# The out-projection of a hybrid decoder layer by seven block products, its weight sums formed beside attention

## The chip, the core and the metric

The kernel runs on one core of one Trainium2 chip. The metric is device time in microseconds (us) of one execution of the whole program. TensorE (PE) multiplies, VectorE (DVE), ScalarE (ACT) and GpSimd (POOL) do the rest of the arithmetic, and SyncE (SP) issues every DMA of this kernel.

## The reference, cut to what matters

One layer on 2048 tokens of width 1024: a norm, one input projection for two groups of heads (latent attention with 8 heads of 64, and a gated linear recurrence of width 512), and then one out-projection of both groups' outputs, the residual and a last norm. All in float32.

```python
h = rms_norm(x, ln_g[l])
proj = h @ w_in[l]
q_lat, kv_lat, k_rope, g_mla, hq, hf, hi, g_hg = jnp.split(proj, split_pts, axis=-1)
y_mla = mla_group(...) * jax.nn.silu(g_mla)                 # (1, 2048, 512)
y_hg = hgrn2_group(...) * jax.nn.silu(g_hg)                 # (1, 2048, 512)
y = jnp.concatenate([y_mla, y_hg], axis=-1) @ w_out[l]      # 2048x1024 by 1024x1024
x = x + y.astype(x.dtype)
return rms_norm(x, final_norm_g)
```

## The kernel before

**Precision.** A float32 product is made of three products of split operands (mm3, lines 67 to 70): each operand is a high part, rounded to the matmul's type, and a low part, the rest. Making the pair takes one cast on ACT and one subtraction on DVE or POOL.

**Stages.** The projections and the recurrence run first (to about 700 us of the span). Attention then runs as 64 steps (line 989): head h, and in it j = 0 to 7, a step for 256 queries. stage_a of a step makes scores in the three "mm" banks of PSUM (lines 881 to 883), DVE negates them and keeps the running maximum, ACT takes the exponential into a row buffer "sn" (line 895). stage_b transposes the rows on PE into a "tp" bank (line 929), splits them into the buffers "ph" and "pl" (932, 933, three of each), multiplies by the values (947, 948) and, in finish, gates the result (953 to 960) and stores it to y_d in DRAM (962). In between POOL scales the gate rows (914, "gp"). The loop at line 1026 merges stage_a of the next step, stage_b of this one, and the preparation of the next head (keys, values, queries, gate rows: lines 783 to 843), which the table of lines 33 to 37 spreads over the steps.

**Buffers.** Tiles with one tag of a pool share its buffers in turn. "gate" (two of 4 KB a partition) holds a head's gate rows, "vp" (two of 8 KB) a head's split values, "qh" and "ql" (two of each) a head's split queries of 512 tokens, "vs" and "ks" the values and keys that are made for several heads at once, "sn" (four of 8 KB) the rows. The pool "lat" holds the latents, the up-projection weights and the keys of even heads; it is closed when they are no longer needed. k_hi1 and k_lo1 hold the keys of odd heads.

**Order.** The text of the program doesn't fix each engine's order. A scheduler of the language places the instructions by a modelled timeline, with the order of the text as priority, and the chip then runs each engine's list in that order. So work from further down can be placed earlier where its inputs and buffers allow.

**Out-projection.** At step 60 (WOUT = 4, line 1030) load_wout (974) closes lat, loads w_out in four pieces into "vp" buffers and splits it: casts on ACT (984), subtractions on POOL (985), one on DVE. After the last step the loop at 1042 takes 16 blocks of 128 tokens: load the block of y_d (1047), split it (1048, 1049), load the residual (1051), and for each half of the 1024 columns sum 8 x 3 products of 512 columns in one bank (1060, 1061), add the residual (1062), square and sum (1063) and multiply by the last gain (1067). Then the scale is made on POOL (1072), both halves are scaled (1073, 1074) and the block is stored. The last block has its second half in two cuts of 256.

Of the kernel before, what the change touches and what calls it, by code (L numbers as in the profile page):

```python
# [37 lines left out]
WOUT = 4  # L38
# [19 lines left out]
def hybrid_kernel(ctx: ExitStack, tc: tile.TileContext, x, x_t, positions, ln_g, w_in, q_a_norm_g, w_q_b,  # L58
# [710 lines left out]
    wk2 = p2.enter_context(tc.tile_pool(name="wk2", bufs=2, side="left"))  # L769
    k_hi1 = big.tile([128, S], F32R, name="k_hi1")  # L770
# [7 lines left out]
    def prep(h):  # L778
# [4 lines left out]
        def start():  # L783
# [4 lines left out]
            hd["gate"] = wk2.tile([128, NBLK, VD], F32, tag="gate", name="gate")  # L788
# [116 lines left out]
    def stage_b(h, j, ctx_, par):  # L905
# [44 lines left out]
        def finish():  # L950
# [6 lines left out]
            tmp = wk.tile([64, 256], F32, tag="oa", name="oa")  # L957
# [16 lines left out]
    def load_wout():  # L974
        p2r.close()
        wo = p2r.enter_context(tc.tile_pool(name="wo", bufs=1, side="right"))
        for k2 in range(KT // 2):
            wr = wk.tile([128, 2, D], F32, tag="vp", name="vp")
            DMA.dma_start(wr, w_out[k2 * 256:(k2 + 1) * 256, :].rearrange("(k p) n -> p k n", p=128))
            for j in range(2):  # L980
                k = 2 * k2 + j
                a = wo.tile([128, D], F32R, name=f"wo_hi{k}")
                b = wo.tile([128, D], F32R, name=f"wo_lo{k}")
                A.copy(a, wr[:, j])
                (V if k == 0 else G).tensor_tensor(b, wr[:, j], f32(a), ALU.subtract)
                w_hi.append(a)
                w_lo.append(b)
# [36 lines left out]
    for i in range(2):  # L1024
        split_q(slice(1024 + 512 * i, 1536 + 512 * i))
    for n, (h, j) in enumerate(seq):
# [3 lines left out]
        if n == (HEADS - 1) * STEPS + WOUT:  # L1030
# [7 lines left out]
    p3 = ExitStack()  # L1038
    op = p3.enter_context(tc.tile_pool(name="op", bufs=2, side="right"))
    fng = wk.tile([128, D], F32, tag="ks", bufs=1, name="ks")  # L1040
    DMA.dma_start(fng, final_norm_g.rearrange("(o n) -> o n", o=1).broadcast_to([128, D]))
    for b in range(NBLK):
        c, r0 = b // 4, b * 128
        t0 = (b % 4) * 128
        yh = op.tile([128, KT, 128], F32R, tag="yh", name="yh")
# [65 lines left out]
```

## Time and profile before

| | us |
|---|---|
| median of 3 runs (1417.76 to 1418.84) | 1418.03 |
| the profiled execution | 1418.87 |
| its span, first to last instruction | 1417.1 |
| PE busy in the span | 1387.7 |
| DVE | 958.6 |
| ACT | 881.2 |
| POOL | 464.8 |

Busy time is a union of modelled spans: matmuls overlap in their pipeline, so PE can read as full while its products come less densely than they could. Counts in a stretch tell more. [...] A line such as L933 is line 933 of the kernel. In a chain of waits each piece is released by the one before it; "issue" is time in which the engine waited for nothing that the profile shows.

### The profile page before, as it was taken

The page shows a single profiled execution, that of the slowest core. Times are in us where ns is not written, and L with a number is a line of the kernel's source. Part 1 is how long each engine was busy: PE and PEld are TensorE (multiplying, and loading weights), DVE is VectorE, ACT ScalarE, POOL GpSimd, SP SyncE. Part 2 cuts the span into 40 slices and gives each one's busy share as a digit, 9 for nine tenths or more (in the row PEclk, how much of TensorE's full clock was granted, in tenths as well). Part 3 has the DMA queues.
Part 4 walks back from the last instruction along what each step waited for, and adds up shares of the span by engine and source line. Part 5 has one row for each costly group of instructions (what it writes and reads, how often), then busy time and mean ns, then how long its engine had stood idle before and what let it go on. Part 6 is the DMA issues. An engine that isn't in the chain of part 4 may idle for free.

```text
span 1417.1 us, 25792 instructions
## 1 busy us (share of the span) xinstructions
PE 1387.7 (98%) x9258; PEld 1263.5 (89%) x9258; DVE 958.6 (68%) x2425; ACT 881.2 (62%) x1796; POOL 464.8 (33%) x635
## 2 busy tenths in 40 slices
PE   8999999999999999999899999999999999999998
PEld 7899879989899988998889898999999998888887
DVE  6547855595845845658388889898889889743333
ACT  6565575456862647355388778778777878732232
POOL 3123613083121622237252425233342525411010
PEclk9999999999999999999989999999999999999999
DMA  7211211215411112111630000100010103244442
GB/s 230 75 48 46 75 53 31 67 42 172 138 46 34 54 52 82 38 42 44 194 73 18 19 22 13 24 13 22 13 26 11 25 22 107 74 144 143 134 148 104
DMA packets 100576, 96.30 MB, mean 68 GB/s; under 512 B 31200, under 2 KB 88800, under 8 KB 100320
## 3 DMA queue, kind: packets, MB, share of 16 engines
q1 hardware_dynamic: 100448, 94.65, 22.7%
q8 instruction: 73, 1.20, 0.4%
q14 instruction: 55, 0.45, 0.1%
HBM read 68.41 MB, written 25.17 MB: 66 GB/s over the span
## 4 chain that ended last, share of the span: by engine, by line
PE 85%; DVE 5%; POOL 3%; ACT 2%; issue 2%; DMA 2%; SPq 0%; POOLq 0%; DVEq 0%; ACTq 0%
PE ps_mm L68 14%; PE ps_mm L69 14%; PE ps_mm L70 14%; PE ps_tp L929 8%; PE ps_a L948 5%; PE ps_a L947 4%; PE ps_mm L881 4%; PE ps_mm L883 4%; PE ps_mm L882 4%; PE ps_b L70 2%; PE ps_b L68 2%; PE ps_b L69 2%; PE ps_a L486 2%; PE ps_b L486 1%; POOL dd L468 1%
## 5 line engine op out<-in xcount | busy, mean ns | idle before, releaser
L68 PE MATMUL ps_mm<-w,hh 128*128 128x256 f32 (+3 forms) x896 | 268.3, 299 | 0.0
L69 PE MATMUL ps_mm<-w,hh 128*128 128x256 f32 (+3 forms) x896 | 263.9, 295 | 0.0
L70 PE MATMUL ps_mm<-w,hl 128*128 128x256 f32 (+3 forms) x896 | 263.0, 294 | 0.0
L933 DVE TENSOR_TENSOR pl<-ps_tp,ph 128x512 fp32r<-128x512 f32 (+1 forms) x288 | 184.6, 655 | 33.3 <-ACT ph L932 32.6
L932 ACT CAST ph<-ps_tp 128x512 fp32r<-128x512 f32 (+1 forms) x288 | 154.4, 565 | 60.2 <-PE ps_tp L929 46.7
L68 PEld LDWEIGHTS ps_mm<-w,hh 128*128 128x128 f32 x896 | 170.1, 190 | 0.7
L69 PEld LDWEIGHTS ps_mm<-w,hh 128*128 128x128 f32 x896 | 169.8, 189 | 0.4
L70 PEld LDWEIGHTS ps_mm<-w,hl 128*128 128x128 f32 x896 | 169.3, 189 | 0.1
L929 PE MATMUL ps_tp<-ident,sn 128*128 128x128 f32 x1088 | 167.9, 274 | 0.8 <-ACT sn L895 0.8
L895 ACT ACTIVATE sn<-sn,mx 128x128 f32<-128x128 f32 (+15 forms) x128 | 154.6, 1208 | 21.2 <-DVE mx L890 20.8
L947 PE MATMUL ps_a<-ph,vp 128*128 128x256 f32 x576 | 155.5, 290 | 0.0
L948 PE MATMUL ps_a<-pl,vp 128*128 128x256 f32 x576 | 147.1, 288 | 0.2 <-DVE pl L933 0.2
L468 POOL TENSOR_TENSOR dd<-G 128x512 f32<-128x512 f32 x80 | 92.8, 1164 | 142.9 <-DVE qd L481 106.9
L929 PEld LDWEIGHTS ps_tp<-ident,sn 128*128 128x128 f32 x1088 | 126.8, 140 | 8.8 <-ACT sn L895 1.3
L881 PE MATMUL ps_mm<-k_hi,qh 128*128 128x512 f32 (+3 forms) x320 | 130.8, 409 | 0.5 <-DVE mx L890 0.2
L886 DVE TENSOR_SCALAR_CACHE_REDUCE sn<-ps_mm,mx 128x512 f32<-128x512 f32 (+3 forms) x192 | 111.5, 581 | 10.9 <-PE ps_mm L883 8.8
L883 PE MATMUL ps_mm<-k_hi,ql 128*128 128x512 f32 (+3 forms) x320 | 116.5, 364 | 1.4 <-DVE ql L842 1.4
L882 PE MATMUL ps_mm<-k_lo,qh 128*128 128x512 f32 (+3 forms) x320 | 116.1, 363 | 0.0
L914 POOL TENSOR_SCALAR gp<-gate,ri 128x64 f32<-128x64 f32 x128 | 56.7, 445 | 180.9 <-DVE ri L897 159.7
L230 DVE SCALAR_TENSOR_TENSOR w<-wr,lng,w 128x256 fp32r<-128x256 f32 (+3 forms) x168 | 89.3, 574 | 39.4 <-ACT w L229 39.4
L948 PEld LDWEIGHTS ps_a<-pl,vp 128*128 128x128 f32 x576 | 109.0, 189 | 6.0 <-DVE pl L933 1.2
L947 PEld LDWEIGHTS ps_a<-ph,vp 128*128 128x128 f32 x576 | 108.9, 189 | 5.8 <-ACT ph L932 0.6
(275 smaller groups left out, 3348.5 us busy)
## 6 DMA issues: line engine op xcount, KB each, us to landing
wr<-in_w_in SPq DMA_DIRECT2D x68, 256.0 KB
yl<-y_d SPq DMA_DIRECT2D x16, 512.0 KB
vp<-in_x SPq DMA_DIRECT2D x16, 512.0 KB
out<-sn SPq DMA_DIRECT2D x15, 512.0 KB
xt<-in_x SPq DMA_DIRECT2D x8, 512.0 KB
xs<-in_x_t SPq DMA_DIRECT2D x8, 512.0 KB
y_d<-yt SPq DMA_DIRECT2D x16, 256.0 KB
gate<-gate_d SPq DMA_DIRECT2D x8, 512.0 KB
```

The source lines that it names most:

```text
L68: PE.matmul(ps, l_hi, r_hi, start=start, stop=False)
L69: PE.matmul(ps, l_hi, r_lo, start=False, stop=False)
L70: PE.matmul(ps, l_lo, r_hi, start=False, stop=stop)
L881: PE.matmul(p[:, :w], qh[:, qs], kh[:, ks], start=True, stop=False)
L882: PE.matmul(p[:, :w], qh[:, qs], kl[:, ks], start=False, stop=False)
L883: PE.matmul(p[:, :w], ql[:, qs], kh[:, ks], start=False, stop=True)
L895: A.activation(sn[:, :nk], sn[:, :nk], AF.Exp, bias=mx[:, kc:kc + 1], scale=-1.0, accum_out=rs)
L929: PE.transpose(tp[:, o:o + 128], prow[i][:, (kb + u) * 128:(kb + u + 1) * 128], ident)
L932: A.copy(ph[:, :w], tp[:, :w])
L933: V.tensor_tensor(pl[:, :w], tp[:, :w], f32(ph[:, :w]), ALU.subtract)
L947: PE.matmul(dst, vv, ph[:, rng], start=st_, stop=False)
L948: PE.matmul(dst, vv, pl[:, rng], start=False, stop=en)
```

## The change

The 1024x1024 weight is seen as 2 x 2 blocks of 512x512, and a pair of 128-token blocks with the two halves of its 1024 inputs as another 2 x 2. The four output blocks are then formed from seven block products and sums (Winograd's form), not eight products. a11 to a22 are blocks of y, b11 to b22 of the weight; s1 to s4 are sums on the y side, t1 to t4 on the weight side.

- **Products.** Pairs of 256 tokens (8 of them). A product has 4 x 3 matmuls of 512 columns. Four banks are held for the whole stage: a, e, b (the mm banks) and c (a tp bank). Product 1 goes to a, which ACT then copies to b; 2 (s1 t1) to e, which is added to both outputs of the second half; 3 (s2 t2) onto b, which ACT copies to c; 4 (a12 b21) onto a, which gives one output; 5 (s3 t3) onto b, another; 6 (s4 b22) onto c; 7 (a22 t4) onto b. Two matmuls ahead of the loop set the banks b and c to accumulate onto what ACT writes.
- **y side.** Each pair loads 1 MB of y_d into a "vp" buffer, forms four sums on DVE and splits seven operands (cast on ACT, subtraction on DVE). a11 and s1 take qh and ql buffers, s2, a12 and a22 take ph and pl, s3 and s4 hold a "gate" buffer each.
- **Weight side.** In steps 16 to 47 (heads 2 to 5) one item a step: load a quarter of the rows and half of the columns of a block, sums on POOL, casts on ACT, low parts on POOL, and stores of the seven split sets to DRAM (14 MB). From step 59 (WOUT = 3) the sets come back, 2 MB each: b11, t1, t2, b21 and t3 where the pool lat was, b22 in the buffers "vs" and "ks", t4 in k_hi1 and k_lo1. load_wout with its splits is gone.
- **Buffers.** "gate" has three buffers, "oa" three, and a new pool "fin" has three of 4 KB.
- **Ends.** The additions, squares, gains, scaling and stores are those of before, now by pairs, written back into the residual's tile; the last product of the last pair runs in two halves.

```diff
-WOUT = 4
+WOUT = 3
+    fin = p2.enter_context(tc.tile_pool(name="fin", bufs=1, side="left"))
...
-            hd["gate"] = wk2.tile([128, NBLK, VD], F32, tag="gate", name="gate")
+            hd["gate"] = wk2.tile([128, NBLK, VD], F32, tag="gate", bufs=3, name="gate")
...
-            tmp = wk.tile([64, 256], F32, tag="oa", name="oa")
+            tmp = wk.tile([64, 256], F32, tag="oa", bufs=3, name="oa")
...
+    ORDER = (("a11", "b11", "a"), ("s1", "t1", "e"), ("s2", "t2", "b"), ("a12", "b21", "a"),
+             ("s3", "t3", "b"), ("s4", "b22", "c"), ("a22", "t4", "b"))
...
+    def wout_sums(kk):
...
+        def load(ch):
+            if ch == 0:
+                o["w"] = wk2.tile([128, 4, 256], F32, tag="gate", bufs=3, name="gate")
+            else:
+                o["w"] = four()
...
+        def sums():
+            w, t = o["w"], four()
+            o["t"] = t
+            G.tensor_tensor(t[:, 0], w[:, 1], w[:, 0], ALU.subtract)
+            G.tensor_tensor(t[:, 1], w[:, 3], t[:, 0], ALU.subtract)
+            G.tensor_tensor(w[:, 1], w[:, 3], w[:, 1], ALU.subtract)
+            G.tensor_tensor(t[:, 2], w[:, 2], t[:, 1], ALU.subtract)
+
+        def split(src, s0, n, ch):
+            ns = slice(ch * 256, ch * 256 + 256)
+            hi = four(F32R)
+            lo = src[:, :n].bitcast(F32R)
+            A.copy(hi[:, :n], src[:, :n])
+            G.tensor_tensor(lo, src[:, :n], f32(hi[:, :n]), ALU.subtract)
+            for i, t in enumerate((hi[:, :n], lo)):
+                DMA.dma_start(f32(w_d[:, s0:s0 + n, i, kk, ns]), f32(t))
...
+    def late_b22():
+        hi = wk.tile([128, S], F32R, tag="vs", bufs=1, name="vs")
+        lo = wk.tile([128, S], F32R, tag="ks", bufs=1, name="ks")
+        wload("b22", flat(hi), flat(lo))
+
+    def late_t4():
+        wload("t4", flat(k_hi1), flat(k_lo1))
...
+        pool, h_, l_, n = (wk, "qh", "ql", 2) if name in ("a11", "s1") else (wk2, "ph", "pl", 3)
...
+        def load():
+            o["raw"] = wk.tile([128, KT, 256], F32, tag="vp", name="vp")
...
+        def total(name, x0, x1, op):
+            t = o["f" + name] = fin.tile([128, 4, 128], F32, tag="ss", bufs=3, name="ss")
+            V.tensor_tensor(t, x0, x1, op)
+            split(name, t)
...
+    for kk in range(4):
+        for k, f in enumerate(wout_sums(kk)):
+            pieces[STEPS * (kk + 2) + k] = [f]
     for n, (h, j) in enumerate(seq):
-        side = [part(*a) for a in plan[n]]
+        side = [part(*a) for a in plan[n]] + pieces.get(n, [])
...
+        first = n - ((HEADS - 1) * STEPS + WOUT)
+        if first == 0:
             run(side)
-            side = []
-            load_wout()
+            side = [open_wout, early("b11")]
+        elif first > 0 and n < len(seq) - 1:
+            side = side + [early(name) for name in {1: ("t1",), 2: ("t2", "b21"), 3: ("t3",)}[first]]
+        elif n == len(seq) - 1:
+            side = pair_operands(0)[:4] + [late_b22, late_t4]
...
+    acc = {"a": mmb(), "e": mmb(), "b": mmb(), "c": tpb()}
+    for key_ in "bc":
+        PE.matmul(acc[key_], wset["b11"][0][:, 0, 0:128], wset["b11"][0][:, 0], start=True, stop=True)
...
+            for k in range(4):
+                first = i < 2 and k == 0
+                PE.matmul(p, ah[:, k], wh[:, k, ns], start=first, stop=False, skip_group_check=True)
+                PE.matmul(p, ah[:, k], wl[:, k, ns], start=False, stop=False, skip_group_check=True)
+                PE.matmul(p, al[:, k], wh[:, k, ns], start=False, stop=k == 3, skip_group_check=True)
...
+        def after(i):
             if i == 0:
+                A.copy(acc["b"], acc["a"])
+            elif i == 1:
+                add(0, H1, acc["e"])
+                add(1, H1, acc["e"])
+            elif i == 2:
+                A.copy(acc["c"], acc["b"])
+            elif i == 3:
+                add(0, H0, acc["a"])
+                done(0, H0, True)
+            elif i == 4:
+                add(1, H1, acc["b"])
+                done(1, H1, True)
+            elif i == 5:
+                add(0, H1, acc["c"])
+                done(0, H1, False)
+                finish(0, H0, H1)
+            elif not last:
+                add(1, H0, acc["b"])
+                done(1, H0, False)
+                finish(1, H1, H0)
...
+    run(pair_operands(0)[4:])
+    for b in range(NBLK // 2):
+        merge(pair_products(b), pair_operands(b + 1) if b + 1 < NBLK // 2 else [])
```

## Rows read from the trace of the kernel before

**Rows 1.** The page, parts 1 and 2: totals of PE, clock in 40 slices

```profile
PE 1387.7 (98%) x9258; PEld 1263.5 (89%) x9258; DVE 958.6 (68%) x2425; ACT 881.2 (62%) x1796; POOL 464.8 (33%) x635
...
PEclk9999999999999999999989999999999999999999
```

**Rows 2.** Busy time by stretch: from:to, length, engines (instructions), clock, DMA share, GB/s

```profile
834.00:1095.00 261.00, 260.98 (x1802) 239.59 (x1801) 225.47 (x721) 210.18 (x441) 94.83 (x145) 1.00 0.08 19
...
1224.00:1260.40 36.40, 36.40 (x214) 31.82 (x212) 16.69 (x33) 15.62 (x33) 5.51 (x9) 1.00 0.23 74
1260.40:1411.20 150.80, 150.51 (x687) 125.41 (x686) 57.19 (x85) 44.11 (x84) 16.97 (x29) 1.00 0.43 141
```

**Rows 3.** Busy time by stretch, instructions on yh alone: PE, weight loads, DVE, ACT

```profile
1224.00:1260.40 36.40, 23.19 (x72) 12.94 (x72) 1.23 (x1) 1.05 (x1) 1.00 0.23 74
...
1260.40:1400.00 139.60, 126.30 (x411) 76.99 (x411) 16.16 (x13) 13.65 (x13) 1.00 0.45 148
```

**Rows 4.** Groups by line and form: busy us, mean ns | idle before, releasers

```profile
L932 ACT CAST ph<-ps_tp 128x512 fp32r<-128x512 f32 x224 | 125.9, 589 | 56.2 <-PE ps_tp L929 43.3 <-PE ps_a L947 10.3
...
L1049 DVE TENSOR_TENSOR yl<-yl,yh 128x1024 fp32r<-128x1024 f32 x16 | 20.1, 1254 | 23.6 <-ACT yh L1048 23.6
L1063 ACT ACTIVATE sn<-vp 128x512 f32<-128x512 f32 x31 | 19.6, 632 | 89.7 <-DVE vp L1062 85.7 <-PE ps_tp L929 4.0
...
L814 POOL TENSOR_TENSOR vp<-vs,vp 128x256 fp32r<-128x256 f32 x24 | 17.4, 737 | 21.8 <-ACT vp L813 21.8
L1048 ACT CAST yh<-yl 128x1024 fp32r<-128x1024 f32 x16 | 16.8, 1050 | 10.4 <-DMA yl<-y_d 10.3
L985 POOL TENSOR_TENSOR wo_lo<-vp,wo_hi 128x1024 fp32r<-128x1024 f32 x7 | 16.8, 2414 | 5.8 <-ACT wo_hi L984 5.8
L1062 DVE TENSOR_TENSOR vp<-ps_mm,vp 128x512 f32<-128x512 f32 x21 | 14.5, 688 | 24.4 <-PE ps_mm L70 23.1 <-DMA vp<-in_x 1.2
...
L1074 DVE SCALAR_TENSOR_TENSOR sn<-vp,rxp,ks 128x512 f32<-128x512 f32 x16 | 12.0, 751 | 10.8 <-POOL rxp L1072 10.8
```

**Rows 5.** Timeline of the end, from 1411.7 us: start, duration, engine and line

```profile
1411.72 0.19 ACT L1063 ACTIVATION_READ_ACCUMULATOR sn<-vp 128x1 f32 x1
```

**Rows 6.** One line's instructions: duration least/median/most, first and last start (w_out's load, cast)

```profile
L979 SPq DMA_DIRECT2D vp<-in_w_out x4: 372/376/379, 1177.3 to 1213.8; - x4
...
L984 ACT CAST wo_hi<-vp x8: 1044/1051/1057, 1185.4 to 1220.2; 128x1024 fp32r<-128x1024 f32 x8
```

**Rows 7.** Chain of waits, 1184 to 1198 us: start, duration, engine and line

```profile
1184.97 0.46 issue
1185.43 0.45 ACT wo_hi L984
...
1185.96 0.42 issue
1186.38 1.06 ACT wo_hi L984
...
1187.51 1.77 POOL wo_lo L985
```

**Rows 8.** Busy time by stretch, around the load of w_out

```profile
1160.00:1180.00 20.00, 20.00 (x149) 18.65 (x148) 16.10 (x51) 15.69 (x35) 5.93 (x10) 1.00 0.12 29
1180.00:1200.00 20.00, 18.91 (x114) 15.53 (x113) 18.52 (x58) 18.14 (x36) 13.13 (x13) 1.00 0.48 151
```

**Rows 9.** Waits of SP's queue, 780 to 1045 us: total, times, longest

```profile
SPq L962 <- POOL oa L960: 202.6, 29, 15.4
```

**Rows 10.** Timeline of PE at the last score; then line 895 from 1210 to 1250 us

```profile
1223.51 0.39 PE L883 MATMUL ps_mm<-k_hi,ql 128*128 128x512 f32 x1
...
1224.10 0.48 PE L68 MATMUL ps_mm<-wo_hi,yh 128*128 128x512 f32 x1
...
L895 ACT ACTIVATE sn<-sn,mx x4: 1714/1852/2007, 1211.1 to 1226.7; 128x1664 f32<-128x1664 f32 x1, 128x1792 f32<-128x1792 f32 x1, 128x1920 f32<-128x1920 f32 x1, 128x2048 f32<-128x2048 f32 x1
```

**Rows 11.** Busy time by stretch, where the projections end

```profile
700.00:720.00 20.00, 13.47 (x55) 10.45 (x54) 14.86 (x33) 14.52 (x29) 13.36 (x14) 0.66 0.99 235
```

More of the change, by code (lines that the diff above doesn't have):

```diff
@@ L972, in hybrid_kernel @@
     w_hi, w_lo = [], []
-    def load_wout():
-        p2r.close()
[L976 to L987, printed above, removed]
+    ORDER = (("a11", "b11", "a"), ("s1", "t1", "e"), ("s2", "t2", "b"), ("a12", "b21", "a"),
+             ("s3", "t3", "b"), ("s4", "b22", "c"), ("a22", "t4", "b"))
@@ new lines, in hybrid_kernel, with wload, four @@
+    wset = {}
+    ys = [{} for _ in range(NBLK // 2)]
+    o_pools = {}
+    SETS = ("b11", "t3", "b21", "b22", "t1", "t2", "t4")
+    w_d = dram.tile([128, 7, 2, 4, 512], F32R, name="wd")
+    def wload(name, hi, lo):
+        wset[name] = (hi, lo)
+        for i, t in enumerate((hi, lo)):
+            DMA.dma_start(f32(t), f32(w_d[:, SETS.index(name), i]))
+    def wout_sums(kk):
+        o = {}
+        def four(dtype=F32):
+            return fin.tile([128, 4, 256], dtype, tag="ss", bufs=3, name="ss")
+        def load(ch):
[4 more added lines that the diff above has]
+            ns = slice(ch * 256, ch * 256 + 256)
+            for g in range(2):
+                r0 = g * 512 + kk * 128
+                DMA.dma_start(o["w"][:, 2 * g:2 * g + 2],
+                              w_out[r0:r0 + 128, :].rearrange("p (c n) -> p c n", c=2)[:, :, ns])
+        def sums():
[6 more added lines that the diff above has]
+        def split(src, s0, n, ch):
+            ns = slice(ch * 256, ch * 256 + 256)
+            hi = four(F32R)
[4 more added lines that the diff above has]
+                DMA.dma_start(f32(w_d[:, s0:s0 + n, i, kk, ns]), f32(t))
+        items = []
+        for ch in range(2):
+            items += [lambda ch=ch: load(ch), sums, lambda ch=ch: split(o["w"], 0, 4, ch),
+                      lambda ch=ch: split(o["t"], 4, 3, ch)]
+        return items
@@ new lines, in pair_operands, with residual, split, quad @@
+    def pair_operands(b):
+        o = ys[b]
+        def load():
+            o["raw"] = wk.tile([128, KT, 256], F32, tag="vp", name="vp")
+            c, t0 = b // 2, (b % 2) * 256
+            DMA.dma_start(o["raw"], y_d[c][:, t0:t0 + 256].rearrange("(k p) t -> p k t", p=128))
+        def residual():
+            xt = wk2.tile([128, 2, D], F32, tag="sn", bufs=4, name="sn")
+            o["x"] = [xt[:, 0], xt[:, 1]]
+            r0 = b * 256
+            DMA.dma_start(xt, x[r0:r0 + 256, :].rearrange("(r p) n -> p r n", p=128))
+        def split(name, src):
+            hi, lo = o[name] = operand(name)
+            A.copy(hi, src)
+            V.tensor_tensor(lo, src, f32(hi), ALU.subtract)
+        def quad(g, i):
+            return o["raw"][:, 4 * g:4 * g + 4, i * 128:(i + 1) * 128]
+        def total(name, x0, x1, op):
+            t = o["f" + name] = fin.tile([128, 4, 128], F32, tag="ss", bufs=3, name="ss")
+            V.tensor_tensor(t, x0, x1, op)
+            split(name, t)
+        return [load, residual, lambda: split("a11", quad(0, 0)),
+                lambda: total("s1", quad(0, 1), quad(1, 1), ALU.add),
+                lambda: total("s2", o["fs1"], quad(0, 0), ALU.subtract),
+                lambda: split("a12", quad(1, 0)),
+                lambda: total("s3", quad(0, 0), quad(0, 1), ALU.subtract),
+                lambda: total("s4", quad(1, 0), o["fs2"], ALU.subtract),
+                lambda: split("a22", quad(1, 1))]
```

106 lines of the change are left out of this document (65 added, 41 removed).

## The prediction

> **What bounds the kernel now.** I read the page's busy shares first, then the busy time by stretch, then the chain that ended last where TensorE (PE) slowed. PE is busy 98% of the span and the clock is full almost throughout [rows 1]. That alone doesn't say which work is worth removing, so I split it by stage [rows 2]. In attention (834 to 1095 us, about where the new weight sums will run) PE reads as full, but DVE is busy 225.5 of 261 us, ACT 210.2 and POOL 94.8: PE, DVE and ACT are nearly balanced, and a delay on one is soon a delay on PE. From 1260 us on it is another kernel: DVE has 57 and ACT 44 of 150.8 us, PE all of it. That is the out-projection alone. So a matmul less there is time saved one for one, as long as the others keep up.
>
> Its rate comes from the same view for the tile yh [rows 3]. Two of every three products read yh, so 411 there are 617 matmuls in 139.6 us: 0.2264 us for one of 512 columns. In the handover, 1224 to 1260 us, 72 stand for 108: 24.5 us of the 36.4 are out-projection, run between the last attention products, and 11.9 us are attention. PE has no gap there.
>
> **Part 1, seven products for eight.** Before, 16 blocks x 2 halves x 8 x 3 = 768 matmuls of 512 columns (the last halves are cut in two, which I count as whole). After, 8 pairs x 7 x 4 x 3 = 672, and two that only open banks "b" and "c". 94 fewer x 0.2264 = **-21.3 us**. A pair then takes 84 x 0.2264 = 19.0 us, a product 2.72 us.
>
> What must fit beside a pair, by [rows 4]: on DVE seven low parts and four sums of 512 elements at half of L1049's 1.254 us, 6.9 us; six additions and two gain products at about 0.69, 5.5; two ends at 0.75, 1.5: 13.9 of 19.0 us. On ACT seven casts at half of L1048's 1.05, 3.7; two bank copies at about 0.59 (the nearest row is L932, which also reads a PSUM bank of 512), 1.2; four squares at 0.63 and a read of their sum at 0.19 [rows 5], 3.3; two ends, taken as on DVE, 1.5: 9.7 us. Neither is the bound. But there is one set of banks, and "a" is copied to "b" and "b" to "c" between products that follow each other by one. Each copy, and the addition that reads "b" before product 7 writes it, has one product, 2.72 us, in which to be done. Behind one other instruction (0.82 on ACT, 0.75 on DVE) a copy or addition ends after 1.4 to 1.5 us, so it is covered; behind three it isn't. No row of before shows a PSUM copy under a product. Bounds: 0 (always covered) to 1.5 us a pair, 12 us (a PE wait as long as one queue item and the copy). A gain is excluded, since nothing was waiting here. I take 0.25 us a pair, near the row where DVE has a quarter of its time free: **+2 us**.
>
> **Part 2, the old weight split goes.** Before, step 60 loads w_out and splits it: eight casts of 1.05 us on ACT [rows 6], seven subtractions of 2.41 on POOL [rows 4]. The chain of waits from 1184.9 to 1197.2 us runs off PE: ACT waits 0.46 us for its load and casts, POOL subtracts, and the small POOL work of attention (gp, ql, oa) stands behind it [rows 7]. What PE lost: its weight loads are busy 15.5 of 20 us there, and 18.65 in the stretch before [rows 8], 3 us of work less. Removed: **-3 us** (bounds 0, if those stalls have other causes, to -4).
>
> **Part 3, the weight sums in heads 2 to 5.** Eight chunks. On POOL each has four subtractions of 256 columns at 0.737, one of 1024 elements at 2.41 and one of 768 at about 1.86 (between the two rows): 7.2 us, 58 in all. On ACT one cast of 1.05 and one of 0.79 (three quarters of it): 14.7 in all [rows 4, 6]. In the 261 us of [rows 2] POOL goes from 36% to 58% and ACT from 81% to 86%; DVE gets nothing. If attention's idle shares absorb it, it costs 0; if every ACT microsecond is paid, 14.7. SP gets 16 loads and 32 stores, moved in front of the y_d stores and the gate rows of the next head. SP already waits in order there (202.6 us of waits for POOL's oa in this stretch [rows 9]) and nobody waits for it, since the y_d rows are read at the end and the gate rows steps later; with three oa buffers instead of two a late store holds up ACT later than now. So the queue itself I cost at nothing. The first load of each head takes a gate buffer that the previous head left; the sums come a step (some 8 us) after it. The nearest row is w_out's own load: issued at 1177.3, the cast that reads it at 1185.4, for twice the bytes [rows 6]. So POOL should mostly find it landed. What stands behind POOL if not: gp, ql and oa, and behind these PE. Price: the old split cost 3 us for 8.4 us of ACT at one place; the new one has 14.7, spread over 32 steps at a load of ACT below the old one's. Bounds: 2 below nothing (a reordering can help) to 14.7; near the small end, because it is spread: **+4 us**.
>
> **Part 4, the handover.** This is where I expect to lose some of it. The last score runs at 1223.51 and the first out-projection matmul at 1224.10 [rows 10], though its first weights were cast from 1185.4 [rows 6]: I read this as mm banks that go out in program order, and expect the same of other shared buffers. After the change the operands s2, a12 and a22 take the ph and pl buffers, in which attention's transposed rows still go round, so they come only when the last groups of step 63 let go. a11 and s1 use qh and ql, free with the last score. So between 1224 us and attention's end PE has products 1 and 2, 24 x 0.2264 = 5.4 us, and 11.9 us of attention: 17.3 us of work, where it had 36.4. Attention's own tail is bound by its chain: the last exponential starts at 1226.7 and takes 2.0 us [rows 10], then eight groups of cast (0.59) and subtraction (0.68). Overlapped that ends near 1237, one after the other near 1240: 13 to 16 us from 1224. So there is nearly enough. Then s2 must be cast and subtracted (1.2 us). Next late: the second pair's y rows, which need the buffer of head 7's values or the first pair's; the load takes up to 8 us as in [rows 6], while products 3 to 7 last 13.6 us. The sets b11 to t3 replace memory that is free when head 7's last queries are made, some steps before the last score; t4 waits for the last score, but product 7 is 16 us behind that. Bounds: 0 to 10 us (a 5 us gap at each of the two places). I take **+2 us**.
>
> The end after the last matmul (add, square, power, scale, store; some 6 us, [rows 5]) keeps its shape and sizes: 0.
>
> **Sum.** -21.3 + 2 - 3 + 4 + 2 = -16.3. The profiled execution took 1418.87 us (span 1417.1, the rest around it), 0.84 over the median of 1418.03. 1418.0 - 16.3 = **1402 us**.
>
> **Rivals.** (A) The chunks are paid in full, slower. The chain of [rows 7] is the price: 0.46 + 0.45 + 0.42 + 1.06 + 1.77 = 4.2 us off PE for one piece of weight work, eight times 33, in place of 4: 1431 us. It decides from 2.5 us a chunk, where 21.3 + 3 - 4 are used up. For it: attention is balanced, and POOL sits idle just because it waits for DVE. Against it: that piece came together with a w_out load, two y casts and the queries of head 7.
> (B) The handover starves: 5 us at s2 and 5 at the second pair, in place of 2: 1410. If the clock falls as well, more: in a stretch of the trace where PE had 6.5 us without work the granted clock is 0.66 over 20 us [rows 11], that is 6.8 us of full speed lost, and 1417 us. [...]
> (C) The bank chain stalls each pair by 1.5 us: 12 in place of 2, 1412 us. For it: order is fixed ahead in each queue. Against: a quarter of DVE and half of ACT is free.
> (D) The saving doesn't arrive, because DVE with its longer work becomes the bound: a pair lasts as long as two blocks did, 21.7 us, 1402 + 21 = 1423 with the other terms. DVE would need 1.6 times its sum; unlikely.
>
> **Chances.** Forecast, 1391 to 1409: 0.60. C: 0.10. B: 0.14. A: 0.13. D: 0.03. Low end: all costs zero and 2 better, 1391. High end: B with the clock, 1418; above it lie A and D, 0.16. A difference under 0.2% (2.8 us, 1415.2 to 1420.9) can't be told from no change. Faster: forecast, C, and half of B, 0.77. Same: the rest of B, 0.07. Slower: A and D, 0.16.
>
> **What would show it.** Right: from some 1250 us a pair each 19 us with 84 matmuls at 0.226 and no wait of PE for ACT or DVE at banks "b" and "c"; no chain through POOL near 1185 us; head 7 reaching its last score within 2 us of 1223.5. Wrong: attention longer by 10 us or more by the last score (A); PE idle for some us between last score and second pair, or a PEclk digit below 9 (B); PE waiting for the PSUM copy once or twice a pair (C); DVE near full in the last stage (D).

## The result, and the profile after

The changed kernel takes **1432.34 us** (median of 4 runs, 1431.46 to 1433.54) where the kernel before takes 1418.06 on the same chip: ratio 1.0086, 95% interval 1.0072 to 1.0100 (the two medians alone give 1.0101). It is slower by 14 us; 1402 had been forecast. The page of its profiled execution, lines of busy time, transfers and chain:

```profile
span 1430.8 us, 25846 instructions
PE 1382.8 (97%) x9152; PEld 1245.8 (87%) x9152; DVE 1006.9 (70%) x2512; ACT 910.0 (64%) x1860; POOL 501.5 (35%) x676
DMA packets 112256, 125.65 MB, mean 88 GB/s; under 512 B 31872, under 2 KB 99712, under 8 KB 110208
PE 72%; DVE 8%; ACT 5%; DMA 5%; POOL 4%; issue 4%; SPq 1%; POOLq 0%; DVEq 0%; ACTq 0%
```

Against [rows 1]: PE has 106 instructions and 5 us of busy time less, in a span that is 13.7 us longer. So the matmuls were saved, and PE then stood idle. Where, stage by stage, is in the table. It is worked out from the starts in the timeline: the first exponential (taken at the load of its table, 1.3 us ahead of it), the last exponential of each head (2048 elements), the last score (which is line 884 after), the first matmul of products 1 and 3 of the first pair, the last matmul. Three things are to be known for reading it. The first exponential comes between 711 and 717 us in kernels that don't differ up to there (713.8 before, 716.0 after), so stages are compared from it on. The kernels were timed in groups, each group on a chip of its own, so a time stands beside that of the kernel before there. And apart from before, after, g3 and g4 each of them ran once, so that a microsecond in the times says little; the stages say more.

```
                      time   before   first   heads   heads   last    products  3 to last  first exp.
                       us    there    exp.    0 to 4  5 to 7  score   1 to 3    matmul     to end
before                1418.06    -     713.8   320.6   192.3   1223.5    -         -         703.3
after                 1432.34 1418.06  716.0   337.9   186.8   1238.8   25.5     158.8       714.8
e1 two chunks         1417.59 1419.15  714.2   325.3   187.6   1225.3   24.1     159.1       701.5
e2 sums held          1426.82 1419.15  711.6   334.9   187.8   1232.3   26.8     158.6       713.4
e3 no casts           1429.0  1419.15  716.4   334.0   186.8   1235.3   24.3     160.4       710.8
e4 sums early         1438.59 1419.15  738.7   320.4   187.4   1244.6   24.6     160.3       698.1
e5 late adds          1430.31 1422.55  711.8   337.3   186.7   1234.0   25.1     161.7       716.7
e6 fixed order        1421.89 1422.55  711.2   338.1   186.8   1234.2   26.5     151.6       708.8
e7 sums early, held   1435.58 1422.55  737.1   320.8   187.5   1243.5   24.5     158.5       696.7
e8 three edits        1438.83 1422.55  738.5   320.4   187.5   1244.6   24.4     160.7       698.6
f1 wf on ACT          1429.17 1419.77  713.9   334.8   187.5   1234.3   26.6     158.9       713.5
f2 no POOL            1429.35 1419.77  713.0   337.3   188.5   1237.0   24.3     159.0       714.6
f3 only transfers     1413.29 1419.77  713.2   322.2   188.5   1222.0   24.6     157.6       698.3
f4 four edits         1416.06 1419.77  716.8   326.2   187.7   1228.8   26.4     151.7       697.5
g4 the same, 4 runs   1411.53 1421.32  716.9   326.1   187.5   1228.5   25.2     151.5       695.6
g1 + sets moved       1406.91 1421.32  711.5   326.0   187.5   1223.1   25.2     149.6       693.6
g2 + additions later  1412.96 1421.32  717.4   326.1   187.6   1229.3   23.1     151.5       693.8
g3 all six, 4 runs    1406.62 1421.32  712.1   326.5   187.6   1224.4   23.1     149.6       692.3
```

**Heads 0 to 4 became 17.3 us longer.** Busy time from 776 to 1058 us, before and then after (PE, PEld, DVE, ACT, POOL, granted clock of PE with 1.00 as full speed, share of the DMA engines, GB/s):

```profile
776.00:1058.00 282.00, 281.98 (x1953) 258.90 (x1951) 242.52 (x779) 226.41 (x480) 105.73 (x161) 1.00 0.09 20
```

```profile
776.00:1058.00 282.00, 274.06 (x1836) 244.77 (x1836) 235.12 (x733) 226.70 (x465) 151.22 (x194) 1.00 0.28 85
```

POOL has 45 us more, but ACT has no more than before and DVE less: 117 matmuls fewer in the same stretch. No engine was out of time; all of them waited. What POOL waited for in 770 to 1080 us (total, times, longest), and what the chain holds at two chunks:

```profile
POOL gp L915 <- DVE ri L898: 70.3, 34, 6.9
...
POOL ss L1013 <- DMA ss<-in_w_out: 11.8, 4, 3.6
```

```profile
778.20 0.46 POOL gp L915
...
778.67 3.27 DMA gate<-in_w_out
...
782.01 0.74 POOL ss L1013
...
783.12 0.74 POOL ss L1014
783.87 0.71 POOL gate L1015
...
923.56 3.22 DMA wd<-ss
...
926.85 4.30 DMA ss<-in_w_out
...
931.26 0.65 POOL ss L1013
```

Behind 923 us the load of a chunk waits for the store that frees its "ss" buffer, then takes 4.3 us itself; POOL's list has reached the sum by then and stands in front of it, and gp, without which no step of attention ends, stands behind.

**The out-projection with its handover saved 1.6 us, not 17.3.** From the last score to the end: 193.6 us before, 192.0 after, and some of attention's work has moved into this stage (part 2 below). PE's instructions in 1280 to 1380 us, before and then after:

```profile
1280.00:1380.00 100.00, 100.00 (x443) 82.81 (x442) 37.93 (x56) 29.72 (x56) 10.70 (x19) 1.00 0.45 145
```

```profile
1280.00:1380.00 100.00, 96.95 (x414) 77.12 (x413) 71.36 (x120) 46.82 (x95) 11.43 (x19) 1.00 0.41 147
```

The same 100 us hold 29 matmuls less, 6.5%, although PE reads only 3% idle: they also follow each other less densely.

### The profile page after: what moved, and what is told of

It is laid out like the page before. It is cut to its first block, busy times and chain, and to the rows that moved or that the text cites. A ratio compares the mean times of both kernels' runs of the same rounds, so it can differ in the third digit from the quotient of the medians.

```text
span 1430.8 us, 25846 instructions
## 1 busy us (share of the span) xinstructions
PE 1382.8 (97%) x9152; PEld 1245.8 (87%) x9152; DVE 1006.9 (70%) x2512; ACT 910.0 (64%) x1860; POOL 501.5 (35%) x676
## 4 chain that ended last, share of the span: by engine, by line
PE 72%; DVE 8%; ACT 5%; DMA 5%; POOL 4%; issue 4%; SPq 1%; POOLq 0%; DVEq 0%; ACTq 0%
PE ps_mm L68 11%; PE ps_mm L69 11%; PE ps_mm L70 11%; PE ps_tp L930 6%; PE ps_a L949 3%; PE ps_mm L882 3%; PE ps_a L948 3%; PE ps_mm L884 3%; PE ps_mm L883 3%; PE ps_mm L1175 3%; PE ps_mm L1177 3%; PE ps_mm L1176 3%; PE ps_a L486 1%; PE ps_b L486 1%; DVE sn L887 1%
```

## Experiments: what the weight sums cost in attention

**One quarter of the sums.** Only the chunks of head 2 are formed; the sets in DRAM hold these rows alone, and the loads of the sets read them four times.

```diff
-            pieces[STEPS * (kk + 2) + k] = [f]
+            pieces[STEPS * (kk + 2) + k] = [f] if kk == 0 else []
```

> The changed kernel with six of the eight weight chunks left out (only the first two are loaded, summed, split and stored; the sets that come back later are filled from these). The four heads during which weight sums run were 17.5 us longer than before (from exponential to exponential). If the sums cause that, six of eight are worth 13 us: about 1419 us, last score near 1226 us. If it is the other buffer counts (gate and oa with three buffers) or another order of attention's own work, nothing changes: 1432 us, last score near 1239.

Heads 0 to 4: 4.7 us over before, not 17.3; from the first exponential to the end it is 13.3 us less than after. The loss in the heads is the sums', by about 2.1 us a chunk (12.6 us for six); the stages behind the last score change little with them.

**Casts left out.** The high parts come from a subtraction on POOL (zeros), the low parts are the loaded rows and the sums as they are, ACT gets nothing.

```diff
-            A.copy(hi[:, :n], src[:, :n])
-            G.tensor_tensor(lo, src[:, :n], f32(hi[:, :n]), ALU.subtract)
+            G.tensor_tensor(hi[:, :n], src[:, :n], src[:, :n], ALU.subtract)
```

> The sixteen casts of the weight chunks on ACT are left out (the high parts are made by POOL as a difference of the same length, so the values are wrong); loads, POOL work and stores stay. Engine-time theory with ACT as the bound: 10 to 15 us back, 1418 to 1422 us. Waiting theory: the POOL list still waits for the loads, at most 4 us back, 1428 to 1432 us.

**POOL's part left out.** No sums and no low parts; what is loaded is cast and stored.

```diff
-            G.tensor_tensor(t[:, 0], w[:, 1], w[:, 0], ALU.subtract)
...
-            G.tensor_tensor(lo, src[:, :n], f32(hi[:, :n]), ALU.subtract)
```

> The changed kernel with POOL's part of the weight items left out (no sums, no low parts; the sets hold wrong values); loads, the sixteen casts on ACT and all stores stay. If POOL is the cause, by its time, by its wait for loads and by what it holds up on VectorE: 10 to 14 of the 17.5 us that heads 1 to 4 lost come back. If ACT's casts (14.7 us) carry half of it: 6 to 9 us back. The run without casts gave 4 us back in these heads.

**Both left out:** 16 loads and 32 stores alone.

> The changed kernel with all arithmetic of the weight items left out; the loads and the stores of the same size stay, as does what is queued on SyncE. If traffic or SyncE's list costs attention anything, it is what remains of the 17.5 us here: I expect 0 to 3 us, so 14 us or more back. If 8 us or more remain, the transfers are a cause of their own.

Heads 0 to 4 over before: 17.3 with all, 13.4 without ACT's part, 16.7 without POOL's, 1.6 without either. So the transfers by themselves, with stores that wait for no engine, cost next to nothing, and the two engines' parts don't add up: either one alone brings most of the loss. Without POOL's part 0.6 us came back, less than either expectation had. That is no sum of busy times. With POOL's work gone it is ACT whose list stands before the load (ACT's waits of f2, 770 to 1080 us, and loads on its chain):

```profile
ACT ss L1016 <- DMA ss<-in_w_out: 6.5, 3, 2.5
```

```profile
784.98 6.09 DMA ss<-in_w_out
791.16 1.78 ACT ss L1016 x2
...
851.77 6.98 DMA ss<-in_w_out
...
922.24 6.10 DMA ss<-in_w_out
```

**The sums held back.** Same work, but an item's instructions are queued, on POOL, behind the latest gp that the text has issued.

```diff
+                mark["gp"] = G.tensor_scalar(out=gp[:, i * 64:(i + 1) * 64],
...
+            def after_gp(f=f):
+                with tc.issue_after(mark["gp"].ins):
+                    f()
-            pieces[STEPS * (kk + 2) + k] = [f]
+            pieces[STEPS * (kk + 2) + k] = [after_gp]
```

> All the work stays; POOL's part of each weight item is queued behind the gate scaling of its own step, so that a load has landed long before POOL comes to it. Waiting theory (POOL's list stands still for loads of w_out, 14 us in all, with attention's small POOL work behind): heads 1 to 5 get 8 to 14 us back, 1418 to 1424 us. Engine-time theory (14.7 us of ACT and 58 us of POOL are what costs): no more than 3 us back, 1429 to 1432 us.

No wait of POOL for w_out is left between 770 and 1080 us, yet only 3.0 us of heads 0 to 4 came back, which the expectation gave to engine time, while e3 came out as it gave to waiting: neither theory alone holds. The chain now named DVE's line 702, two tensor_scalar of 96 columns on the query weights, with 3.3 us:

```profile
864.92 0.85 ACT ss L1023
...
865.79 0.37 SPq L1026
...
866.20 0.03 SPq L700
...
866.26 3.07 DMA wf<-in_w_q_b
...
869.43 3.33 DVE wf L702 x2
```

The upper rows are a third list that stands in order: SP issues the load of the query weights behind a store of a weight set, which waits for its cast on ACT. In the changed kernel line 702 reads (min, median, longest ns), and around 877 us DVE and then POOL did:

```profile
L702 DVE TENSOR_SCALAR wf<-wf,gq x14: 257/490/2971, 713.8 to 1078.8; 128x96 f32<-128x96 f32 x14
```

```profile
877.33 3.21 DVE L702 TENSOR_SCALAR wf<-wf,gq 128x96 f32<-128x96 f32 x2 [0.63 <-DMA wf<-in_w_q_b]
880.46 0.68 DVE L839 TENSOR_TENSOR qf<-ps_mm,csT 128x512 f32<-128x512 f32 x1
```

```profile
876.40 1.28 POOL L843 TENSOR_TENSOR ql<-qf,qh 128x512 fp32r<-128x512 f32 x1
877.64 1.83 POOL L1023 TENSOR_TENSOR ss<-ss 128x768 fp32r<-128x768 f32 x1
879.44 0.72 POOL L961 TENSOR_TENSOR oa<-oa,og 64x256 f32<-64x256 f32 x1
```

In the kernel before, the same 14 instructions take 254 to 690 ns. Here the longest lasts 2.97 us, until POOL's chain of three, the low part of a weight set among them, is through. So it is 0.26 us at the shortest and 2.97 us under POOL, through three instructions one right behind the other. With POOL's part left out (f2) the longest is 0.68 us again. By what POOL's work holds DVE there is not shown by any view.

**That line on ACT.**

```diff
-            V.tensor_scalar(out=wf[:, k, 0:96], in0=wf[:, k, 0:96], scalar1=gq[:, k:k + 1], scalar2=None,
-                            op0=ALU.mult)
+            A.activation(wf[:, k, 0:96], wf[:, k, 0:96], AF.Copy, scale=gq[:, k:k + 1])
```

> The changed kernel with one edit: the two scalings of a head's query weights (wf, 96 columns, 0.25 us each) are made by ACT instead of VectorE. In the changed kernel VectorE took up to 2.97 us for one of them, while POOL ran a weight subtraction of 2.4 us; before, at most 0.69. Summed over heads 1 to 4 the pairs took 7.8 us against 2.3. If VectorE stands still there for POOL's hold on SBUF, and its list with it: 4 to 6 us back in these heads. If the long ones merely sit in time that VectorE had to spare: no more than 1 us back.

3.1 us in heads 0 to 4. Held sums and this together give 11.7 (f4 and g4, below; their other edits come into play only behind the heads), nearly twice 3.0 + 3.1. Part of the difference is the clock. In e2 PE waited 2.77 us, for work that stood behind line 702, and from near the end of that wait the granted clock was 0.50 for 6.8 us:

```profile
873.48 0.58 PE L883 MATMUL ps_mm<-k_hi,qh 128*128 128x256 f32 x1 [2.77 <-DVE sn L888]
```

```profile
872.80:879.60 6.80, 6.12 (x24) 5.76 (x25) 5.40 (x16) 1.12 (x4) 1.57 (x4) 0.50 0.59 187
```

In the kernel before, matmuls of 512 columns start every 0.43 us at a clock of 0.50 (714.93 to 716.64 us) and every 0.23 at 1.00 (699.66 to 700.58). From that, 6.12 us of work at 0.50 are some 3 us lost, by my estimate, which neither the changed kernel nor f4 loses there. (e3 and f2 have 3.4 us at 0.50 in these heads, up to 1.7 us lost in each.) The rest I read as one stall hiding part of the other; no run parts them further.

**The sums before attention.** The items run beside the projections, in buffers that are idle there; in e7 they are also queued behind a late instruction of POOL and of SP.

```diff
...
+    WS = [f for kk in range(4) for f in wout_sums(kk)]
-    merge(U[7:], lat_q(0, hA))
+    merge(U[7:], lat_q(0, hA), WS[:12])
-    merge(U[:16], vv + gg)
+    merge(U[:16], vv + gg, WS[12:])
```

> The same weight sums, moved ahead into the first half of the projection stage, in three buffers that are idle there; attention has none. If attention, with PE, DVE and ACT balanced, is what makes them dear: its heads go back to 63 to 67 us, and the projections, where ACT and DVE are half busy, lose 0 to 5 us: 1415 to 1420 us. If the work or its 28 MB of traffic costs the same anywhere: 1430 to 1434 us.

> The weight sums in the projection stage again, but each item queued on POOL and on SyncE behind the work that precedes it in the text, so that they can't be drawn ahead to the first 100 us, where the loads of x and w_in share the DMA engines and the work before them cost 25 us. If that drawing ahead was the price: projections end 2 to 8 us later than before instead of 25, attention as before, 1415 to 1421 us. If the projections have no room for the work (POOL's differences there are waited for by ACT): still 15 us or more late, 1428 us or more.

Heads 0 to 4 are then as before (320.4 us), but attention begins 25 us later, 23 in e7, more than either expectation of e4 allowed. The first 100 us, before and then e4:

```profile
0.00:100.00 100.00, 94.69 (x571) 82.60 (x572) 55.16 (x118) 64.78 (x113) 21.94 (x43) 0.97 0.43 125
```

```profile
0.00:100.00 100.00, 87.55 (x479) 72.33 (x479) 58.21 (x105) 62.53 (x102) 52.50 (x68) 0.95 0.66 205
```

The scheduler drew the sums to the very beginning (POOL 52.5 for 21.9 us), where the projections' own weights are being loaded, and PE got 92 matmuls less. Held back, they lose the same at 100 to 300 us (e7: 678 and 629 matmuls in these two stretches of 100 us, for 715 and 765 before). A place that is free in engine time isn't free in order and in transfers. e8 (e7's edit with the late additions and the fixed order of the next section) ended the same. Its 160.7 us from product 3 on, in spite of the fixed order, hold one wait of PE of 6.3 us for an addition in the first pair, where the late additions have the fault told below, and 6.8 us at a clock of 0.50 around its end.

> The edits of the three runs ahead of this one together: sums held in the projections, late additions, fixed order of products. If they cost and gain apart from each other: 1432 less 13, less 5, less 6, some 1408 us, and below the kernel before by 10. If one hides the other (the time lost at the handover covers that of the first pairs): 1413 to 1418 us.

## Experiments: the pairs and the handover

PE's waits in the pair stage of the changed kernel (1264 to 1424 us), and a piece of its chain:

```profile
PE ps_mm L1177 <- DVE ql L1084: 2.7, 4, 0.7
PE ps_mm L1175 <- ACT ps_mm L1214: 1.8, 1, 1.8
PE ps_mm L1175 <- ACT ps_tp L1219: 1.0, 1, 1.0
```

```profile
1323.79 0.26 DVE sn L1181
...
1324.39 0.69 DVE ql L1084
...
1325.13 0.51 PE ps_mm L1177
```

Products of two pairs change places here: by the scheduler's modelled timeline product 2 of the next pair, and product 1, go ahead of product 7 of the pair. DVE's list then holds the addition that waits for product 7 in front of the low part that product 2 needs.

**A fixed order of products.** Each product is queued on PE behind the one before it in the text.

```diff
+            if "pe" in mark_pe:
+                with tc.issue_after(mark_pe["pe"].ins):
+                    product_(i, ns)
...
```

> The changed kernel with the products of the out-projection queued on TensorE strictly in the order of the text; the scheduler had moved product 2 of the next pair and product 7 of the last across each other, and then the low part of s1 stood on VectorE behind an addition that waits for product 7. Order theory: the waits of 1.1 us in pairs 4 to 7 and 2.1 us in pair 8 go, some 6 us in all: 1425 to 1428 us. Bank-chain theory (the copies themselves need longer than a product): waits stay or grow, 1431 us or more. The pitch of a matmul, 0.233 us where before had 0.227, stays with either.

From product 3 to the last matmul 151.6 us, 7.2 less, and a single wait of PE is left:

```profile
PE ps_mm L1184 <- DVE sn L1190: 0.5, 1, 0.5
```

So the bank copies themselves are covered, as reasoned; the order was the loss. The two waits for a copy that the changed kernel had (1.8 and 1.0 us) went with it.

**The handover.** The chain of the changed kernel there:

```profile
1253.52 6.41 DMA sn<-in_x
...
1260.56 0.68 DVE sn L1181
1261.24 0.61 DVE pl L934
1261.89 0.39 PE ps_a L949
```

The first pair's residual rows wait for a row buffer, and the addition that reads them stands in DVE's list in front of attention's last subtractions. Between products 1 and 3 PE has one wait of note:

```profile
PE ps_a L949 <- DVE pl L934: 2.2, 1, 2.2
```

In e5 the first pair's two additions of product 2 were moved two products later in the text. In it and in e8 the first pair's product 2 then falls through to the last branch, by which the second block of that pair is also added and scaled once too often, so it says little:

```diff
-            elif i == 1:
+            elif i == 1 and b:
                 add(0, H1, acc["e"])
                 add(1, H1, acc["e"])
...
             elif i == 3:
+                if b == 0:
+                    add(0, H1, acc["e"])
+                    add(1, H1, acc["e"])
```

> The changed kernel with one edit: the first pair adds its product 2 to the residual two products later. In the handover VectorE came to this addition at 1257 us, the residual's rows landed at 1260, and the last subtractions of attention stood behind it, and behind these TensorE. If that queue is what the handover lost: product 3 starts 4 to 7 us earlier after the last score (19 to 22 us behind it instead of 26), 1425 to 1428 us. If product 3 waits for the ph and pl buffers in any case: no change, 1431 to 1433 us.

25.1 us from product 1 to product 3, where it was 25.5. f4 has the move without that fault, and the scheduler still put the addition first (PE's wait is 1.9 us there), so the order of the text is not the lever.

## Experiments: the edits together

f4 joins the held sums, line 702 on ACT, the later additions and the fixed order.

> A kernel with the whole arithmetic and four edits to the changed one: wf scaled on ACT, sums held to their own steps, the first pair's additions of product 2 two products later, products in fixed order on TensorE. If the shares add: 5 (wf), 3 (held), 5 (additions), 6 (order): some 19 us below the changed kernel and 4 to 6 us below the kernel before on this chip. If the late additions change nothing in the handover: level with the kernel before, within 2 us.

> The kernel of f4_four_edits again, timed in three rounds: one look gave 1416.1 beside 1419.8 of before. If that gain is real, the ratio is 0.996 to 0.999 with an interval below 1; if it was the start of attention that differed by chance, the interval holds 1.

Timed, it is 1411.53 us for 1421.32: 0.9933, interval 0.9914 to 0.9952. Two causes were still open. **The first additions**, now queued on DVE behind the low part of a22, and thus behind attention's last subtraction:

```diff
+            mark["lo"] = V.tensor_tensor(lo, src, f32(hi), ALU.subtract)
...
+                    with tc.issue_after(mark["a22"].ins):
+                        add(0, H1, acc["e"])
+                        add(1, H1, acc["e"])
...
+    mark["a22"] = mark["lo"]
```

> The kernel of f4_four_edits, with the first pair's two additions from bank e queued on DVE behind the first pair's last low part (a22), so that they no longer stand in DVE's list ahead of attention's last subtractions and of s2. If the late residual rows in front of that list were the handover's loss, the time from the first to the third product falls from 26.5 us to about 18 to 21 (17.3 us of work, and a gap at s2 of up to 3), and the end with it: 1409 to 1413. If another chain ends the handover (attention's own tail, the y rows), it stays above 24 and the time at about 1416.

23.1 us from product 1 to 3, for 25.2: between the two expectations. PE's wait is gone; in g3, with the same edit, its longest there is 0.2 us. So what is left is hardly a wait: it is more work of attention than was counted. The groups of subtractions around and behind the last score, in the kernel before and then in g3 (count; ns; first and last start):

```profile
L933 DVE TENSOR_TENSOR pl<-ps_tp,ph x14: 550/681/692, 1223.0 to 1255.3; 128x512 fp32r<-128x512 f32 x12, 128x384 fp32r<-128x384 f32 x2
```

```profile
L934 DVE TENSOR_TENSOR pl<-ps_tp,ph x18: 547/691/693, 1230.1 to 1247.5; 128x512 fp32r<-128x512 f32 x15, 128x384 fp32r<-128x384 f32 x3
```

18 groups are still to be done then, and as many in after, e1, e6, f3, f4 and the other kernels of g. They follow each other by (1247.5 - 1230.1) / 17 = 1.02 us, and from product 1 to 3 PE is busy for 22.9 of the 23.2 us. On PE it is the same: products with the values behind the last score, in the kernel before and then in the changed one (the second number is PE's, with its count):

```profile
1223.90:1260.50 36.60, 9.84 (x60) 8.77 (x60) 0.83 (x2) 0.74 (x2) 1.00 0.23 74
```

```profile
1239.26:1266.00 26.74, 13.82 (x84) 11.36 (x84) 1.22 (x3) 1.11 (x3) 1.00 0.49 175
```

With the transposes it is 107 instructions of attention before and 144 after.

**The pitch.** With a fixed order the pairs had no gap and yet 432 matmuls in 100 us where the kernel before has 443. By the program's allocation, all operands and weights of the out-projection begin there 32 bytes off a multiple of 64 in a partition; after, the five sets of the right-hand area do, and the operands and the other two sets (b22, t4) don't. An unused tile moves these sets by 32 bytes:

```diff
+        p2r.enter_context(tc.tile_pool(name="pad", bufs=1, side="right")).tile([128, 8], F32, name="pad")
         o_pools["wo"] = p2r.enter_context(tc.tile_pool(name="wo", bufs=1, side="right"))
```

> The kernel of f4_four_edits, with an unused tile of 32 bytes a partition ahead of the early weight sets, so that the five sets of the right-hand area begin on a multiple of 64 bytes, as the operands qh, ql, ph and pl already do; before, sets and operands alike began 32 bytes off such a multiple and a matmul came every 0.2267 us, in f4 the five sets are off and the operands are not, and it is 0.233 to 0.235. If what counts is that both lie alike, the pitch of these five falls to about 0.227 and the end comes 480 x 0.0065 = 3 us sooner than f4 (1413). If the place has nothing to do with it, it stays at 0.233 to 0.235 and the time within 1.5 us of 1416.

g4 and then g1, 1280 to 1380 us:

```profile
1280.00:1380.00 100.00, 100.00 (x433) 80.90 (x432) 71.57 (x118) 48.07 (x98) 10.91 (x21) 1.00 0.41 140
```

```profile
1280.00:1380.00 100.00, 100.00 (x438) 82.01 (x437) 71.27 (x119) 49.22 (x101) 11.34 (x21) 1.00 0.37 127
```

Half of the difference to 443 is back, 1.9 us of the stage, where 3 were expected; g3 against g2, which differ by the same edit, gives 1.9 again. By product it is clearer. From a product's first matmul to that of the next one, over pairs 2 to 7, the matmuls of products 2 to 5, whose sets moved, come every 0.2333 us in g4 and 0.2288 in g1 or g3. Product 7, whose set t4 stayed, has 0.2267 in all three, which is the pace of the kernel before. Product 6, whose set b22 stayed too, has 0.2299 in g4 and 0.2308 in g1. So the place of a set matters, but a multiple of 64 under both tiles isn't the whole rule. Of the 7.4 us between the two profiled executions (1414.32 and 1406.91) another 5.3 are an earlier first exponential, which e2, e5 and e6 have without this edit.

> Both of the edits above in the kernel of f4_four_edits. If the list of causes (waiting in order in heads 0 to 4, DVE under POOL, the pair order, the handover, the pitch) is complete enough, 1407 to 1411 on a chip where the kernel before takes 1418 to 1420, some 0.6% faster. If the two new edits have nothing, about 1416, 0.2% faster.

All six edits: **1406.62 us for 1421.32, ratio 0.9904, interval 0.9888 to 0.9921**. It takes 11.0 us less than the kernel before from the first exponential to the end (692.3 for 703.3).

## Why the prediction was wrong, point by point

**Part 1, seven products: the count was right, its rate was not.** 674 matmuls came. (A product in two halves is counted as one.) But they were priced at the rate of the old code. From start to start a matmul takes 0.2321 us in e6 and 0.2267 in the kernel before: 0.0054 on each of the 648 from product 3 on, 3.5 us over the 146.7 that they would take at 0.2264. No bound had been set on it.

**The bank chain, +2 (0 to 12): its size was inside the bounds, its mechanism was not.** 7.2 us (158.8 to 151.6, e6), from products in another order than the text's; the two waits for a bank copy came of that order. The argument "between products that follow each other by one" took the order of the text for the order of the list, which the scheduler makes from a modelled timeline. Rival C named this stage, with 12 us; as a mechanism it fell.

**Part 2, the old split, -3: no gain is shown.** Heads 5 to 7 are 5.5 us shorter, 4.8 of it in head 7, which looks like the forecast. But less work lies in them. From the last exponential of head 6 to that of head 7, before and then after:

```profile
1163.30:1226.70 63.40, 62.30 (x412) 55.13 (x412) 56.29 (x175) 54.30 (x103) 34.54 (x34) 1.00 0.29 93
```

```profile
1182.10:1240.70 58.60, 57.41 (x366) 49.46 (x366) 52.14 (x171) 42.38 (x85) 15.51 (x25) 1.00 0.53 207
```

PE has 46 instructions less there, and 37 of attention's more behind the last score (107 to 144, above). At the prediction's 11.9 us for 106 of them [rows 2, 3] these are some 4 us, by my estimate. e4, whose heads 0 to 4 are as before, has 58.5 us in head 7 as well. From the last exponential of head 4 to the last product with the values, it is 226.1 us before, with 107 of the out-projection's matmuls in it, and 212.0 after, with 29; less these at 0.2264 us, attention takes 201.9 and 205.4. What the split's removal gave can't be seen in that, and why more is left behind the last score stays open. The 0.46 us of "issue" in [rows 7] were also no wait of ACT for its load: it was casting for attention (line 932, 0.59 us from 1184.95).

**Part 3, the weight sums, +4 (-2 to 14.7): the step that failed.** They cost 17.3 us. Two things were passed over. The cost was taken from engine time, with ACT's 14.7 us as the upper end. f4 keeps all of that work, holds the sums back, moves line 702 to ACT, and loses 5.6 us: so 11.7 of the 17.3 are not engine time but waiting in order, behind a load that comes late, and holding. "POOL should mostly find it landed", said the prediction from the one load of [rows 6]; POOL found it missing four times for 11.8 us. And "DVE gets nothing" was true of its list and false of its time: line 702 was held under POOL for up to 2.97 us. How the 11.7 divide between the two, and what the last 5.6 are, is not shown: with either engine's part left out most of the loss stays, in e3 without POOL's wait for the "ss" loads. Rival A was the right one, at half its price: 17.3 / 8 = 2.2 us a chunk, where it took 4.2 from [rows 7]; it said it would decide from 2.5 a chunk, with everything else as forecast. That its 1431 us lie beside the measured 1432 is luck: the rest of the way came from the other parts.

**Part 4, the handover, +2 (0 to 10): the work in it was mis-counted.** 25.5 us passed between products 1 and 3, where the prediction put 17.3 us of work: 8.2 us. Some 4 of these are the work of attention that heads 5 to 7 no longer have (part 2), a shift and not a loss. 2.1 are the residual rows in front of DVE's list (g2, and PE's wait of 2.2 us); the prediction looked for a late load at the second pair's y rows instead. The last 2 us stay in g3, where no wait of PE is over 0.2 us; they are open. The prediction took eight groups of cast and subtraction to be left after the last score; [rows 10] show one exponential, not the groups, and their count, in the rows above, was 14 before and is 18 after. Rival B had 10 us here, from gaps of PE at two places, and more if the clock fell as well. In the changed kernel there is one gap, of 2.2 us, and the clock stayed at 1.00; but in e2, e6, f1 and f4 it was 0.50 for 3.4 us in this handover, and f4's 26.4 us beside g4's 25.2, the same kernel, are the nearest to a price of that.

**The sum.** -21.3 + 3.5 (pace of a matmul) + 7.2 (order) - 5.5 (heads 5 to 7) + 17.3 (sums) + 8.2 (handover) = +9.4. Of the -5.5 and the 8.2 some 4 us are one and the same work. With 1.3 us by which the last score comes later against head 7's last exponential, and 0.7 behind the last matmul, it is 11.4 of the 11.5 from first exponential to end (714.8 - 703.3). The other 2.2 us of the 13.7 are the later first exponential. The forecast was 16 us of gain. g3 gains 14.7 as timed and 11.0 from the first exponential to the end; what is left of the sums there, 5.9 us, is about what it lacks.

## What to carry to other kernels

Price side work in a full stage by what stands behind it in each engine's list while its input is late, not by busy time: find the load, what frees its buffer, and the instruction of the critical loop that follows. Where a scheduler orders the lists by a model, read the order in the trace before costing a hand-written overlap, and pin the few instructions that matter with an explicit order. Before a new owner takes an engine's idle time, look at which other engine's instructions grow longer under it (here DVE's line 702, from 0.26 to 2.97 us). And where stages are divided at a marker such as the last score, count the instructions on both sides: work that moves across it reads as a gain in one stage and a loss in the next.

## What the runs showed of the hardware

A tensor_scalar of 128x96 on DVE took 2.97 us, not 0.26, while POOL worked through three instructions (line 702, changed kernel, 877.33 us), and with POOL's part left out at most 0.68 (f2); by what POOL's work holds it is not shown. Matmuls of 512 columns, all at a granted clock of 1.00, came every 0.2267 us with all tiles 32 bytes off a multiple of 64 (before), every 0.2333 with weight sets off and operands on it (products 2 to 5 of g4) and every 0.2288 with both on it (the same products of g1); product 7, with both on it in either kernel, kept 0.2267. That the place matters is shown by g1 against g4 and g3 against g2; why, and what the rule is, is not. PE read as 97% busy in 1280 to 1380 us of the changed kernel with 6.5% fewer matmuls than before. And from near the end of a gap of 2.77 us on PE (e2) the granted clock was 0.50 for 6.8 us.
